# Decay exponents as a bias, a gating norm on another engine, and the order of the last tiles

## The chip, the cores and the metric

The program runs on one core of a Trainium2 chip. The metric is device time in microseconds. The kernel before took 1852.29 us, the median of 3 runs (1849.40 to 1852.42). Engine names are those of the profile: PE is TensorE, DVE is VectorE, ACT is ScalarE, POOL is GpSimd, SP is the engine that issues most DMAs. Each has its own instruction queue and works it off in order.

## The reference

One block of a streaming encoder on a sequence of 1024 rows with 1024 channels, all in float32:

```
x = x + 0.5 * SwiGLU_1(RMSNorm(x))             # hidden width 2816
h = RMSNorm(x);  p = h @ W_in                  # u, v (512 each), q, k, v, z, beta, a
    y_a = gelu(u) * (W_s . layernorm(gelu(v)) + b_s)    # 8 groups of 64 channels, blocks of 128 rows
    y_b = RMSNorm(gated_delta_rule(q, k, v, beta, g)) * silu(z)   # 4 heads of 128, chunks of 64 rows
x = x + concat(y_a, y_b) @ W_out
x = x + 0.5 * SwiGLU_2(RMSNorm(x))
y = RMSNorm(x)
```

Two pieces matter here. In the gated delta rule `decay[i, j] = exp(g_i - g_j)` where j is at or before i, and zero elsewhere, with g the running sum of the gates in a chunk; it is used once below the diagonal (in the matrix L, which a triangular solve inverts) and once with the diagonal (for the attention of the queries). In the spatial gating each row of gelu(v) is normed over its 512 channels, scaled and shifted by `gm_ln_g` and `gm_ln_b`, then mixed over the rows by W_s, and b_s is added.

## The kernel before

Rows stand in tiles of 128 (the partitions), so there are 8 tiles, 0 to 7. Products of float32 are made from a high and a low part in another format: a CAST on ACT makes the high part, a subtraction on DVE the low part (`split`, line 61 and 62, and like lines), and each product takes three matmuls (`mm3`, line 53). A program builder takes the kernel's text and sets, with a cost model of its own, the order in which each engine gets its instructions; the text's order and buffers bound it, and what an engine has been given it works off in that order. So an edit in one place moves instructions elsewhere.

The kernel has three parts. The two feed-forward parts (`ffn`) form products of weight and activation sums on PE, in `plan` order, with hidden values written to DRAM (`hq`) and read back as `left`, and weight sums (`wq`) read back as `right`; `unit` is one such pair, cast and split. The last step of the plan ends four tiles at once: `ev` adds a result into the tile `x` (DVE, line 332), and `emit` norms it. In the first part `emit` is `to_mid` (its result `xn` is transposed by PE), in the second it is `fin`, which writes `o` to the output. Both use `rstd_of` (lines 72 to 78): Square with a sum on ACT, a multiply and add on DVE, a power of -0.5 on POOL (`rpow`, line 70).

The middle part does the mixing. In order of the text:

- `v0` projects half of v; beside it `decay(h)` (lines 786 to 803) makes, for each of four heads, `EL` and `EA`, two tiles E of 128 x 2 x 512. `grb` is the row of g, loaded from DRAM to all partitions into one of four buffers; `gc` is g as a column; `csa` holds the masks (0 or -1e30).
- `keys(h)` projects the keys (`proj_conv`: matmuls into `mm`, a copy to `pad` on ACT, a convolution in four DVE passes into `acc`, Silu on ACT into `kst`), transposes them on PE (`ax<-ident,kst`), norms them (`rk`) and forms L with EL. `fill` puts steps of another projection between.
- `substitute` is the triangular solve for all blocks: 31 steps of two DVE operations each (aT, then X), one behind the other. X is written to DRAM (`xz`) and read back as Z and X by `Half.load`; the PE then needs Z for `inverse`.
- The second half of v is projected; its eviction `ev_v` applies Gelu, and `mix` norms a tile: statistics on DVE, the power on POOL, two DVE passes over 128x512 (lines 1083 and 1084). `spatial` mixes two tiles (a pair) on PE (`ax<-vm,u`), adds b_s on DVE (line 1094) and stores to DRAM. The tiles `vm` and X share three buffers, so the load of pair 2 waits for the store of pair 0.
- The scan over chunks, head by head, with the projections of the next head between.

ACT needs a table load (`ACT_TABLE_LOAD`) when it goes from one kind of function to another: Exp, Silu and Gelu each need one here, copies, casts and Square come without.

## Time and profile before

| what | value |
|---|---|
| median of 3 runs | 1852.29 us (1849.40 to 1852.42) |
| the profiled execution | 1841.22 us, its span 1839.4 us |
| granted PE clock over the span | 0.992 |
| PE busy | 1784.1 us, 97% |
| DVE busy | 1191.7 us, 65% |
| ACT busy | 686.6 us, 37% |
| POOL busy | 747.9 us, 41% |

The span is from the first to the last instruction of the one profiled execution; its own time is 1.8 us longer, and the runs' median 11 us longer than that. Shares are averages over stages that differ: the first feed-forward part lasts until about 700 us, the middle part until about 1080, the second feed-forward part to the end. In a row such as `745.78 5.92 PE ... x35 [2.75 <-DVE wk L62]` the first number is the start in us, the second the length, x35 the merged instructions, and the bracket is how long the engine stood idle before and what ended that. In a row with `679/686/1781` these are the shortest, median and longest duration in ns. In a row of `a:b` the numbers are, for that stretch, the busy time of PE, PEld (weight load), DVE, ACT and POOL, then the clock, the DMA share and GB/s.

### The profile page before, as it was taken

What the parts mean: (1) busy time and instruction counts of PE and PEld (TensorE: products, weight loads), DVE (VectorE), ACT (ScalarE), POOL (GpSimd) and SP (SyncE); (2) the same over time, 40 slices, a digit from 0 to 9 for tenths busy, and PEclk for the clock granted to TensorE, in tenths of its full rate; (3) what the DMA queues carried; (4) which work ended last, traced back from release to release, by engine and by line L of the source; (5) the groups of instructions that cost most, each with busy time, mean ns of one, the idle gap of its engine ahead of it and who ended that gap; (6) DMA issues with size and microseconds to landing.
All of it is one profiled execution on the core that took longest, in us unless ns stands there. A gap on an engine that the chain in (4) does not pass through costs nothing.

```text
span 1839.4 us, 25484 instructions
## 1 busy us (share of the span) xinstructions
PE 1784.1 (97%) x9735; PEld 1524.8 (83%) x9735; DVE 1191.7 (65%) x1531; ACT 686.6 (37%) x1193; POOL 747.9 (41%) x583
## 2 busy tenths in 40 slices
PE   5999999999999999898999999999999999999997
PEld 4888888888788889797788989988888888878886
DVE  6867676665565575769655344587776766656546
ACT  6333332333343454432344533452333323243433
POOL 4667666565140012212132420366666665614001
PEclk9999999999999999999999999999999999999999
DMA  5353443544957445453432254334535445495744
GB/s 196 108 175 136 162 152 134 184 158 163 339 188 258 155 177 164 140 195 100 133 94 67 90 197 136 109 104 165 178 132 171 144 154 188 142 344 185 264 142 149
DMA packets 134441, 302.26 MB, mean 164 GB/s; under 512 B 27408, under 2 KB 42032, under 8 KB 134320
## 3 DMA queue, kind: packets, MB, share of 16 engines
q1 hardware_dynamic: 131824, 296.20, 46.9%
q10 hardware_dynamic: 2496, 4.44, 0.8%
q8 instruction: 76, 1.25, 0.3%
q14 instruction: 45, 0.37, 0.1%
HBM read 208.83 MB, written 91.77 MB: 163 GB/s over the span
## 4 chain that ended last, share of the span: by engine, by line
PE 78%; DVE 8%; DMA 5%; POOL 4%; issue 3%; ACT 2%; SPq 0%; POOLq 0%; DVEq 0%; ACTq 0%
PE mm L53 43%; PE ax L53 32%; POOL s L191 1%; POOL t L278 1%; DMA left<-hq 1%; DVE acc L873 1%; PE ax L95 1%; PE sd L53 1%; DMA graw<-in_f1gu_dram 1%; POOL s L278 1%; PE sc L53 1%; DVE T L119 0%; DVE unit L62 0%; DVE wk L62 0%; DVE E L797 0%
## 5 line engine op out<-in xcount | busy, mean ns | idle before, releaser
L53 PE MATMUL mm<-unit 128*128 128x512 f32 x1056 | 244.9, 392 | 4.2 <-ACT unit L61 2.2
L53 PEld LDWEIGHTS mm<-unit 128*128 128x128 f32 x1056 | 198.8, 189 | 47.4 <-ACT unit L61 3.3
L191 POOL TENSOR_TENSOR s<-graw 128x512 f32<-128x512 f32 x84 | 130.3, 1551 | 262.9 <-DMA graw<-in_f2gu_dram 116.0
L62 DVE TENSOR_TENSOR ga<-graw,ga 128x512 fp32r<-128x512 f32 x134 | 155.9, 1166 | 99.9 <-ACT ga L61 99.2
L61 ACT CAST gs<-s 128x512 fp32r<-128x512 f32 x168 | 104.5, 622 | 301.8 <-PE mm L53 151.0
L62 DVE TENSOR_TENSOR unit<-left,unit 128x1024 fp32r<-128x1024 f32 x84 | 101.9, 1215 | 133.0 <-ACT unit L61 132.3
L53 PE MATMUL ax<-T,gs 128*128 128x512 f32 x792 | 183.1, 389 | 0.0
L53 PE MATMUL ax<-unit 128*128 128x512 f32 x792 | 180.5, 389 | 0.0
L53 PEld LDWEIGHTS ax<-T,gs 128*128 128x128 f32 x792 | 148.7, 188 | 30.8
L53 PEld LDWEIGHTS ax<-unit 128*128 128x128 f32 x792 | 148.7, 188 | 30.8
L62 DVE TENSOR_TENSOR gs<-s,gs 128x512 fp32r<-128x512 f32 x168 | 172.7, 1030 | 2.3
L53 PE MATMUL mm<-B,ga 128*128 128x512 f32 (+1 forms) x864 | 166.8, 347 | 3.3 <-ACT B L118 1.9
L61 ACT CAST unit<-left 128x1024 fp32r<-128x1024 f32 x84 | 82.5, 982 | 230.2 <-PE ax L53 100.5
L53 PE MATMUL mm<-T,gs 128*128 128x512 f32 x720 | 166.5, 389 | 0.0
L53 PEld LDWEIGHTS mm<-B,ga 128*128 128x128 f32 x864 | 139.5, 194 | 23.4 <-ACT B L118 2.5
L53 PEld LDWEIGHTS mm<-T,gs 128*128 128x128 f32 x720 | 135.2, 188 | 28.0
L70 POOL TENSOR_TENSOR rs<-rs,half 128x1 f32<-128x1 f32 (+1 forms) x29 | 19.2, 662 | 334.5 <-DVE rs L76 334.4
L53 PE MATMUL mm<-actT,wk 128*128 128x512 f32 x576 | 150.4, 403 | 0.0
L53 PE MATMUL ax<-B,ga 128*128 128x512 f32 x528 | 127.2, 390 | 1.4 <-DVE ga L62 1.4
L53 PE MATMUL mm<-wk,actT 128*128 128x256 f32 x960 | 123.5, 285 | 2.7 <-DVE wk L62 2.7
L53 PEld LDWEIGHTS mm<-wk,actT 128*128 128x128 f32 x960 | 117.4, 190 | 3.4 <-DVE wk L62 3.0
L53 PEld LDWEIGHTS mm<-actT,wk 128*128 128x128 f32 x576 | 103.6, 188 | 18.8
(239 smaller groups left out, 3046.0 us busy)
## 6 DMA issues: line engine op xcount, KB each, us to landing
left<-hq SPq DMA_DIRECT2D x70, 512.0 KB, 5.0
graw<-in_f1gu_dram SPq DMA_DIRECT2D x44, 512.0 KB, 5.4
wq<-t SPq DMA_DIRECT2D x44, 512.0 KB, 2.8
hq<-s SPq DMA_DIRECT2D x44, 512.0 KB, 3.1
graw<-in_f2gu_dram SPq DMA_DIRECT2D x44, 512.0 KB, 4.7
right<-wq SPq DMA_DIRECT2D x40, 512.0 KB, 4.8
wd<-in_f1wd_dram SPq DMA_DIRECT2D x22, 512.0 KB, 6.6
hq<-sg SPq DMA_DIRECT2D x22, 512.0 KB, 3.7
```

The lines of the kernel that those rows point to most:

```text
L53: nc.tensor.matmul(*args, **kw)
L61: nc.scalar.copy(h, src)
L62: nc.vector.tensor_tensor(l, src, h, op=ALU.subtract)
L70: nc.gpsimd.tensor_tensor(o, i, half[:, :w], op=ALU.pow)
L95: nc.tensor.transpose(ps[:, i * P:(i + 1) * P], blk(i), ident)
L191: nc.gpsimd.tensor_tensor(f, u, v, op=op)
L278: nc.gpsimd.tensor_tensor(o, u, v, op=op)
L873: nc.vector.scalar_tensor_tensor(acc, pad[:, j:j + 512], cw[:, blk, j:j + 1], acc, op0=ALU.mult, op1=ALU.add)
```

## The change

1. Decay: E now holds only mask minus, or plus, the row g, formed in one operation; the column g goes in as the bias of the Exp, which therefore runs on 128 columns at a time. The Exps of EA are placed behind each head's keys.
2. Gating norm: the norm of v is one ACT pass with a bias and a scale column; the channel weights `gm_ln_g` are applied behind the mixing (DVE), and the shift C (from `gm_ln_b`, W_s and b_s) is added there by POOL. C is formed once in `gm_shift`. `gm_consts` moves ahead of `substitute`.
3. The reciprocal root (`rsqrt`) is an addition and a power, both on POOL, with the division by n in the Square's scale; it replaces a DVE operation in `rstd_of`, the keys' norm and `mix`.
4. Last tiles: tile 6's product is returned as a function, to be called later, and tile 7's two halves change places.

```diff
     def rpow(o, i, w):
         nc.gpsimd.tensor_tensor(o, i, half[:, :w], op=ALU.pow)
+    def rsqrt(o, i, add, w=1):
+        nc.gpsimd.tensor_scalar(o, i, add, None, op0=ALU.add)
+        rpow(o, o, w)
     def rstd_of(src, junk, n):
         ms = sm.tile([P, 1], F32, tag="ms", name="ms", bufs=4)
-        nc.scalar.activation(junk, src, AF.Square, accum_out=ms)
+        nc.scalar.activation(junk, src, AF.Square, scale=n ** -0.5, accum_out=ms)
         rs = sm.tile([P, 1], F32, tag="rs", name="rs", bufs=4)
-        nc.vector.tensor_scalar(rs, ms, 1.0 / n, EPS, op0=ALU.mult, op1=ALU.add)
-        rpow(rs, rs, 1)
+        rsqrt(rs, ms, EPS)
         return rs
...
         def fin(t, xt):
             o = gp.tile([P, D], F32, tag="gsp", name="o", bufs=7)
             if t < 7:
-                normed(xt, st["gf"], o)
-                nc.sync.dma_start(odram[t], o)
-                return
-            halves = slice(0, 512), slice(512, D)
+                rs = rstd_of(xt, o, D)
+                def scaled():
+                    nc.vector.scalar_tensor_tensor(o, xt, rs, st["gf"], op0=ALU.mult, op1=ALU.mult)
+                    nc.sync.dma_start(odram[t], o)
+                if t == 6:
+                    return scaled
+                return scaled()
+            halves = slice(512, D), slice(0, 512)
...
     EL, EA = {}, {}
+    ngc = na
+    nc.vector.tensor_scalar(ngc, gc, -1.0, None, op0=ALU.mult)
     def decay(h):
...
-            nc.vector.tensor_tensor(av_, v4(grb), b4(gc[:, cs]), op=ALU.subtract)
-            eng = nc.vector if hf else nc.gpsimd
-            eng.tensor_tensor(lv_, mask(C_ML), v4(grb), op=ALU.subtract)
-            eng.tensor_tensor(lv_, lv_, b4(gc[:, cs]), op=ALU.add)
-            nc.scalar.activation(lv_, lv_, AF.Exp)
-            nc.vector.tensor_tensor(av_, av_, mask(C_MA), op=ALU.add)
-            nc.scalar.activation(av_, av_, AF.Exp)
+            for e, i, eng, op in ((EL[h], C_ML, nc.vector if hf else nc.gpsimd, ALU.subtract), (EA[h], C_MA, nc.vector, ALU.add)):
+                eng.tensor_tensor(v4(e[:, hf]), K(i).unsqueeze(1).to_broadcast([P, 4, P]), v4(grb), op=op)
+
+    def exponents(e, bias, h):
+        for hf in range(2):
+            for t in range(4):
+                c = h * 8 + hf * 4 + t
+                nc.scalar.activation(e[h][:, hf, tl(t)], e[h][:, hf, tl(t)], AF.Exp, bias=bias[:, c:c + 1])
...
-            rk = inv_norm(ssk, 1.0, EPS, "k")
+            rk = small("rk")
+            rsqrt(rk, ssk, EPS, 4)
...
+    def gm_shift(gm):
+        _, C, bs, wsT = gm
+        rows_ = bank(ps_a, "ax")[:, :8]
+        for g in range(8):
+            mm(rows_[:, g:g + 1], wsT[g // 4][:, g % 4], ones, start=True, stop=True)
+        rw = bs[:, 8:16]
+        nc.scalar.copy(rw, rows_)
+        for g in range(8):
+            c = C[:, g * 64:g * 64 + 64]
+            nc.scalar.activation(c, c, AF.Identity, bias=bs[:, g:g + 1], scale=rw[:, g:g + 1])
     def mix(t, v, gm):
...
-        nc.vector.tensor_scalar(rs, mv[:, 1:2], EPS, None, op0=ALU.add)
-        rpow(rs, rs, 1)
-        nc.vector.scalar_tensor_tensor(v, v, mv[:, 0:1], lng, op0=ALU.subtract, op1=ALU.mult)
-        nc.vector.scalar_tensor_tensor(v, v, rs, lnb, op0=ALU.mult, op1=ALU.add)
+        rsqrt(rs, mv[:, 1:2], EPS)
+        nm = mv[:, 0:1]
+        nc.gpsimd.tensor_scalar(nm, mv[:, 0:1], rs, -1.0, op0=ALU.mult, op1=ALU.mult)
+        nc.scalar.activation(v, v, AF.Identity, bias=nm, scale=rs)
     def spatial(t, Vs, gm):
...
-            nc.vector.tensor_tensor(
-                Vs[:, :, gh * 256:gh * 256 + 256].rearrange("p t (g c) -> p g t c", g=4),
-                mp.rearrange("p (g t c) -> p g t c", g=4, t=2),
-                gm[2][:, gh * 4:gh * 4 + 4].unsqueeze(2).unsqueeze(3).to_broadcast([P, 4, 2, 64]), op=ALU.add)
+            o = Vs[:, :, gh * 256:gh * 256 + 256].rearrange("p t (g c) -> p g t c", g=4)
...
+            nc.vector.tensor_tensor(o, mp.rearrange("p (g t c) -> p g t c", g=4, t=2), each(lng), op=ALU.mult)
+            nc.gpsimd.tensor_tensor(o, o, each(C), op=ALU.add)
...
     for h in range(HEADS):
         decay(h)
+        exponents(EL, gc, h)
         together(islice(v0, 2))
...
         keys(h, fill)
+        exponents(EA, ngc, h)
     together(fill)
+    gm = gm_consts()
+    gm_shift(gm)
     substitute()
-    gm = gm_consts()
```

**What the order makes of it.** First place: ACT at the end of the decay and the first head's keys. E are the exponents, wk<-raw the high parts of projection weights, kst<-acc the Silu that ends the convolution of one half of the keys. Before:

```order
L61 CAST wk<-raw 128x1024
L801 ACTIVATE E<-E 128x512
L803 ACTIVATE E<-E 128x512
L801 ACTIVATE E<-E 128x512
L803 ACTIVATE E<-E 128x512 x2
L869 COPY pad<-mm 128x512
L801 ACTIVATE E<-E 128x512
L875 ACT_TABLE_LOAD
L875 ACTIVATE kst<-acc 128x512
L869 COPY pad<-mm 128x512
L61 CAST wk<-raw 128x1024
L896 ACTIVATE kst,ssk<-ax 128x128
```

And of the change (gc is the bias of EL, na that of EA):

```order
L61 CAST wk<-raw 128x1024
L876 COPY pad<-mm 128x512
L810 ACTIVATE E<-E,na 128x128 x12
L882 ACT_TABLE_LOAD
L882 ACTIVATE kst<-acc 128x512
L876 COPY pad<-mm 128x512
L61 CAST wk<-raw 128x1024
L810 ACT_TABLE_LOAD
L810 ACTIVATE E<-E,na 128x128 x7
L882 ACT_TABLE_LOAD
L882 ACTIVATE kst<-acc 128x512
L903 ACTIVATE kst,ssk<-ax 128x128 x8
```

The last Exps of the decay no longer all stand ahead of the first Silu: seven stand between the two Silus of the first head and five more behind them, with a load on either side. Over the program ACT has 20 loads instead of 16.

Second place: PE from the second half of v to the first use of Z. Before:

```order
L53 MATMUL mm<-wk,actT 128x256 x128
L53 MATMUL ax<-vm,u 128x128 x8
L53 MATMUL mm<-wk,actT 128x256 x40
L53 MATMUL ax<-vm,u 128x128 x8
L53 MATMUL mm<-wk,actT 128x256 x24
L53 MATMUL mm<-actT,wk 128x512 x38
L53 MATMUL ax<-vm,u 128x128 x8
L53 MATMUL mm<-actT,wk 128x512 x23
L53 MATMUL ax<-vm,u 128x128 x8
L53 MATMUL mm<-actT,wk 128x512 x83
L53 MATMUL sq<-S,wq 128x128
L53 MATMUL mm<-actT,wk 128x512 x36
```

Of the change:

```order
L53 MATMUL mm<-wk,actT 128x256 x105
L53 MATMUL ax<-vm,u 128x128 x8
L53 MATMUL mm<-wk,actT 128x256 x32
L53 MATMUL ax<-vm,u 128x128 x8
L53 MATMUL mm<-wk,actT 128x256 x42
L53 MATMUL mm<-actT,wk 128x512 x6
L53 MATMUL ax<-vm,u 128x128 x8
L53 MATMUL mm<-actT,wk 128x512 x42
L53 MATMUL ax<-vm,u 128x128 x8
L53 MATMUL mm<-actT,wk 128x512 x96
L53 MATMUL sq<-S,wq 128x128
L53 MATMUL mm<-actT,wk 128x512 x8
```

Ahead of the change's first row stand 13 more of the same and the eight matmuls of `gm_shift`; the row behind each list is the first with Z. The mixings (ax<-vm,u) move forward by 10, 18, then 32 matmuls of 512 columns less, and 152 matmuls of 512 columns stand ahead of Z instead of 180. On POOL, between the norms of the pairs, the change has this (brs and bmv are a tile's scale and bias, the row of vm the two additions of C for one pair):

```order
L74 TENSOR_SCALAR brs<-bmv 128x1
L70 TENSOR_TENSOR brs<-brs,half 128x1
L1102 TENSOR_SCALAR bmv<-bmv,brs 128x1
L1118 TENSOR_TENSOR vm<-vm,rv 128x4x2x64 x2
L74 TENSOR_SCALAR brs<-bmv 128x1
```

The additions of one pair stand ahead of the first operation of the next pair's norm.

Third place: SP in the last step of the plan, where left is read for the last units and o is written. Before:

```order
L648 DMA out_dram<-o 128x1024
L377 DMA left<-hq_10683 128x1024
L648 DMA out_dram<-o 128x1024
L377 DMA left<-hq_10684 128x1024
L648 DMA out_dram<-o 128x1024 x2
L377 DMA left<-hq_10685 128x1024
L377 DMA left<-hq_10686 128x512
L648 DMA out_dram<-o 128x1024 x3
L661 DMA out_dram<-o 128x512
```

Of the change:

```order
L655 DMA out_dram<-o 128x1024
L381 DMA left<-hq_10742 128x1024
L655 DMA out_dram<-o 128x1024 x3
L381 DMA left<-hq_10743 128x1024
L381 DMA left<-hq_10744 128x1024
L381 DMA left<-hq_10745 128x512
L655 DMA out_dram<-o 128x1024 x3
L669 DMA out_dram<-o 128x512
```

The second left now stands behind the outputs of tiles 1 to 3. On DVE the end of the program reads, before, x, o, x, o, x, o, x and the two halves of tile 7; with the change x, x, o, o, x, o, x and the halves: tile 6's product still stands ahead of tile 7's x.

24 lines of the change are left out of this document (11 added, 13 removed).

## The prediction

> **What bounds the kernel now.** I read the page's head first, then who TensorE waits for, then the two stages that the change touches as busy time and in order of time.
>
> ```profile
> span 1839.4 us, 25484 instructions
> PE 1784.1 (97%) x9735; PEld 1524.8 (83%) x9735; DVE 1191.7 (65%) x1531; ACT 686.6 (37%) x1193; POOL 747.9 (41%) x583
> ```
>
> TensorE stands still for 1839.4 - 1784.1 = 55.3 us. The change adds eight matmuls of one column to its work, so it can win or lose only where TensorE waits. TensorE's waits, first between 700 and 765 us (decay and first keys), then between 800 and 900 us (gating norm and triangular solve); columns are total, times, longest:
>
> ```profile
> PE mm L53 <- DVE wk L62: 2.7, 1, 2.7
> PE ax L844 <- ACT kst L875: 2.2, 1, 2.2
> ...
> PE ax L53 <- DVE vm L1084: 4.4, 3, 2.9
> PE ax L53 <- issue: 1.2, 1, 1.2
> PE ax L53 <- DMA Z<-xz: 1.2, 1, 1.2
> ```
>
> These 5 and 6.8 us are what the two large edits can reach. VectorE is nearly full in both stretches (22.75 of 23.00 and 39.93 of 41.83 us):
>
> ```profile
> 722.00:745.00 23.00, 21.03 (x134) 18.92 (x133) 22.75 (x25) 12.18 (x22) 12.27 (x8) 1.00 0.31 97
> 841.00:882.83 41.83, 40.37 (x212) 34.18 (x211) 39.93 (x93) 13.09 (x21) 8.32 (x9) 1.00 0.35 122
> ```
>
> **Decay.** Removed: eight subtractions and eight mask additions on VectorE become eight additions, four of its eight other operations go, and POOL loses four (24 to 12 on VectorE, 8 to 4 on POOL). Added: 64 exponentials of 128 columns for 16 of 512, and, by the order, four table loads, since half of the exponentials now stand between the keys' Silus.
>
> ```profile
> L797 DVE TENSOR_TENSOR E<-grb,gc x8: 679/686/1781, 722.2 to 741.5; 128x512 f32<-128x512 f32 x8
> L799 POOL TENSOR_TENSOR E<-csa,grb x4: 1530/1760/1818, 722.2 to 735.6; 128x512 f32<-128x512 f32 x4
> L1040 ACT ACTIVATE ax<-oh,rq 128x128 f32<-128x128 f32 x32 | 11.9, 372 | 2.4 <-DVE oh L1037 1.8
> 730.99 1.15 ACT L801 ACTIVATE E<-E 128x512 f32<-128x512 f32 x2 [1.08 <-DVE E L800]
> L875 ACT ACT_TABLE_LOAD x2 | 2.6, 1283 | 0.0
> 741.34 1.69 PE L53 MATMUL mm<-wk,actT 128*128 128x256 f32 x13
> 745.78 5.92 PE L53 MATMUL mm<-wk,actT 128*128 128x256 f32 x35 [2.75 <-DVE wk L62]
> 755.52 0.66 PE L844 MATMUL ax<-ident,kst 128*128 128x128 f32 x4 [2.25 <-ACT kst L875]
> ```
>
> No row shows an Exp with a column of biases; the nearest is the Square with a column of scales (L1040), 0.37 us. Two Exps of 0.63 us take 1.15 us, so neighbours overlap by 0.1: 0.27 us each, 64 x 0.27 = 17.3 us against 16 x 0.575 = 9.2. With 4 x 1.28 us of loads, ScalarE gains 13 us of work. If the bias costs nothing it is 0.18 each, the lower bound.
>
> When are the last E ready? POOL's four take 4 x 1.76 = 7.0 us from 722.25; beside them VectorE gets about one operation per 1.5 us, five in all; seven more at 0.69, and a microsecond for the last grb, whose buffer comes free late: 735.3 instead of about 744.6. ScalarE then has, in the new order, four exponentials 1.1, a cast 1.05, eight 2.2, a cast 1.05, the copy of pad 0.6, twelve 3.2, a load 1.28, Silu 0.63: the first kst at 746.4. Then copy 0.6, cast 1.05, load 1.28, seven 1.9, load 1.28, Silu 0.63: the second at 753.1. TensorE finds its wk in time (the casts end at 737.5 and 740.7; VectorE is free), so the 2.75 us go; it waits only for the second kst, and starts those transposes at 753.2 instead of 755.52 with five more matmuls of 0.23 us behind it: 755.5 - 753.2 + 1.2 = **3.5 us won**. Bounds: 5.0 (both waits gone) and 0.5 (ScalarE 3 us later).
>
> [...]
>
> ```profile
> 708.29 1.28 ACT L761 ACT_TABLE_LOAD   x1
> 709.58 0.23 ACT L761 ACTIVATE na<-na 128x32 f32<-128x32 f32 x1
> ```
>
> **Gating norm.** Sixteen VectorE passes of 0.75 us (L1084 below is one) go. In their place ScalarE makes eight passes (0.63 us and the columns: about 0.8), POOL eight small operations more, and, after the mixing, eight additions of 128x512 that follow the product on VectorE. In the order POOL makes both additions of one pair of tiles before it starts the next pair's norm.
>
> ```profile
> L70 POOL TENSOR_TENSOR brs<-brs,half x8: 758/1177/1247, 828.1 to 860.5; 128x1 f32<-128x1 f32 x8
> 815.81 13.82 PE L53 MATMUL mm<-wk,actT 128*128 128x256 f32 x116
> 830.85 2.02 PE L53 MATMUL ax<-vm,u 128*128 128x128 f32 x16 [1.22 <-issue]
> 840.48 2.02 PE L53 MATMUL ax<-vm,u 128*128 128x128 f32 x16 [2.89 <-DVE vm L1084]
> 854.63 2.02 PE L53 MATMUL ax<-vm,u 128*128 128x128 f32 x16 [0.66 <-DVE vm L1084]
> 864.47 19.09 PE L53 MATMUL mm<-actT,wk 128*128 128x512 f32 x83
> 893.16 0.41 PE L53 MATMUL ax<-Z,L 32*32 32x32 f32 x8 [1.17 <-DMA Z<-xz]
> 840.62 0.36 DVE L920 TENSOR_TENSOR aT<-Lb,X 128x192 f32<-128x192 f32 x1
> 849.96 0.75 DVE L1084 SCALAR_TENSOR_TENSOR vm<-vm,brs,rv 128x512 f32<-128x512 f32 x1 [0.43 <-POOL brs L70]
> 882.83 0.33 SPq L923 DMA_DIRECT2D xz<-X  x1
> 820.28 1.28 ACT L1108 ACT_TABLE_LOAD   x1 [4.51 <-PE mm L53]
> ```
>
> TensorE, in before's clock: the new order lets it reach the first mixing ten matmuls earlier, at 828.4; the norm (aggregate at 828, two POOL chains of 0.27 + 0.6 + 0.27, ScalarE 0.8) is done near 831.2: it waits 2.8 (before 1.2). It reaches the second at 836.8; POOL has the first pair's additions until 836, then two chains: 840.4, wait 3.6 (before 2.9). Before the third it needs the low part of a wk that VectorE now makes after six of the solve's operations, two products and two statistics, near 850.2: wait 2.6 (before 0.7). The fourth: none (before 0.8). Sum 9.0 against 5.6.
>
> Behind that stands the solve, a chain on VectorE alone, whose X goes through DRAM: stored at 882.83, and used by TensorE at 893.16, 10.3 us later. In the new order 28 matmuls of 0.23 us, 6.5 us, that ran ahead of this wait stand behind it. So to lose nothing TensorE must pass it at 893.2 - 6.5 = 886.7. Without any wait it would be there at 881.4 (from 815.81: 192 x 0.119, four mixings of 1.8, 152 x 0.23, and 0.6 for the short ones), with 9.0 at 890.4. And X? From 840.62 to 882.83 VectorE takes 42.2 us. Eight passes less their overlap, four waits of 0.43 and four small operations go, 7.3; two convolution passes move behind it, 1.3; dependent neighbours close up, 0.6 back: 34.2 us from 841.4, so 875.6 if POOL leaves VectorE alone. It does not: while POOL ran its six decay operations VectorE's 0.69 us operations took up to 1.78, and six of them needed 8.7 us instead of 3.6, 0.85 us lost for each of POOL's. Six additions lie in this stretch: 5.1, so 880.7, and TensorE gets Z at 891.0. **Lost: 891.0 - 886.7 = 4.3 us.** Bounds: won 0.6 (X at 875.6, the waits 6.1), lost 8.2 (each addition holds VectorE 1.5 us: X at 884.6).
>
> [...]
>
> **The rest.**
>
> ```profile
> 1822.08 0.15 DVE L76 TENSOR_SCALAR rs<-ms 128x1 f32<-128x1 f32 x1 [1.22 <-ACT o L74]
> 1834.06 0.19 POOL L657 TENSOR_SCALAR rs<-rs 128x1 f32<-128x1 f32 x1
> 640.00:680.00 40.00, 40.00 (x197) 33.37 (x197) 30.51 (x40) 21.63 (x33) 4.21 (x6) 1.00 0.40 145
> ```
>
> rs on POOL: the small VectorE operation (0.15 us) becomes one of POOL of 0.19 that stands 0.27 before the power; from Square to product 0.99 for 0.91 us. About four of these lie on TensorE's way (head, second half's start): +0.3. At the end of the first half TensorE never waits between 640 and 680 us, but three x now go ahead of xn on VectorE: +0.2 (0 to 1). The shift of C (eight passes of 64 columns, about 2.4 us) lies in a stretch in which ScalarE waits 4.5 us (820.28): nothing; without that cover, 2.4.
>
> The last tiles:
>
> ```profile
> 1805.17 0.43 SPq L377 DMA_DIRECT2D left<-hq  x1
> 1808.42 1.29 DVE L82 SCALAR_TENSOR_TENSOR o<-x,rs,grow 128x1024 f32<-128x1024 f32 x1 [0.66 <-POOL rs L70]
> 1811.30 1.05 ACT L61 CAST unit<-left 128x1024 fp32r<-128x1024 f32 x1 [0.47 <-DMA left<-hq]
> 1824.16 0.69 DVE L332 SCALAR_TENSOR_TENSOR x<-mm,x 128x512 f32<-128x512 f32 x1
> 1830.99 1.28 DVE L82 SCALAR_TENSOR_TENSOR o<-x,rs,grow 128x1024 f32<-128x1024 f32 x1 [0.73 <-POOL rs L70]
> 1832.19 0.68 DVE L332 SCALAR_TENSOR_TENSOR x<-mm,x 128x512 f32<-128x512 f32 x1
> ```
>
> The order moves only tile 5's x ahead of tile 4's o; tile 6's o still stands ahead of tile 7's x. x of tile 5 comes at 1823.6 instead of 1824.2, and the chain behind it ends 0.4 earlier. But on SP the second left now stands behind the o of tile 3: issued near 1809.0 instead of 1805.2, cast near 1814.8 instead of 1811.3, and needed by TensorE, through cast and subtraction, near 1816.7: +0.8 (0 to 1.5). Together +0.4.
>
> **Sum.** -3.5 + 4.3 + 0.3 + 0.2 + 0.4 = +1.7 us, on the span 1839.4 to 1841.1. The profiled execution took 1841.22 us, 1.8 around its span; the runs' median is 1852.29, 11 us more, so I put the difference on the median: **1854.0 us**.
>
> **Rivals.** *Slower:* POOL's additions hold VectorE for their whole length, the solve ends at 884.6, TensorE starves for Z: +8.2 there, in all +5.6, 1857.9; with the decay's gain at its lower bound +8.6, 1860.9. For it: the E rows and VectorE's 95% in that stretch. Against: VectorE gets in between. It decides from X stored later than 883. *Faster:* the additions fall into VectorE's own waits, X at 875.6: -0.6 there, -4.5 in the decay, nothing at the ends: about -5, 1847. For it: VectorE loses 20 us of work in two stretches that it fills. Against: VectorE stands in order behind TensorE's mixing, which is late. *The last tiles are not reordered as said:* the order shows so; it is in the sum, and if tile 7's x did go first, another 1.4 us would be won.
>
> **Numbers.** 0.2% is 3.7 us, about what can be told from no change. Forecast (the two terms about cancel) 0.39; slower rival 0.36; faster rival 0.25. The range reaches to both: 1844 (both large terms at their best, and 3 us of noise between runs, which spread by that) to 1861. The likeliest case alone: 1850 to 1857.
>
> **What would show it.** Right: the wait on wk near 745 gone, the one on the second kst left at 1 to 3 us; ScalarE's 128x128 Exps near 0.37 us; mixing waits together 7 to 10 us; a wait for Z of up to some microseconds, X stored near 881; VectorE's two-input operations longer beside POOL's additions. Wrong: TensorE waiting for banks or fill behind ScalarE in the decay (then slower), or X stored before 877 and mixing waits under 5 us (then faster).

## The result: 14 us slower, outside the range

| | before | after |
|---|---|---|
| median | 1849.04 us (1842.73 to 1865.67) | 1862.98 us (1856.85 to 1871.34) |
| the profiled execution | 1841.22 us | 1862.39 us |
| its span, clock | 1839.4 us, 0.992 | 1860.5 us, 0.983 |

The ratio is 1.0073, with a 95% interval of 1.0056 to 1.0090: 13.5 us slower, 10.4 to 16.6. The forecast was 1854.0 us, the range ended at 1861. It was put on 1852.29 us, the median of the first three runs of before; with all twenty this median is 1849.04. So the miss is larger in the difference than in the time: +1.7 us were forecast, 13.5 measured. The profiled execution of before lies near the low end of its runs; so the traces differ by 21.1 us where the medians differ by 13.9. The page of after begins:

```profile
span 1860.5 us, 25590 instructions
PE 1799.0 (97%) x9751; PEld 1534.5 (82%) x9751; DVE 1157.8 (62%) x1461; ACT 710.1 (38%) x1262; POOL 764.7 (41%) x638
```

TensorE is still busy for 97%. Of the 21.1 us its idle time makes 6.2 (61.5 us instead of 55.3) and its busy time 14.9, though its work is the same but for eight one-column matmuls. The granted clock of both traces is at every instant 1.00 or 0.50 (in after 1.00 over 880 to 892 us, 0.50 over 896 to 904). A mean of 0.992 is then about 29 us at 0.50 (2 x 0.008 x 1839.4), and one of 0.983 about 63 (2 x 0.017 x 1860.5). These 34 us more at half the clock are up to 17 us of lost work, so waits alone do not explain the result.

TensorE's waits of after, first between 700 and 765 us, then between 800 and 900 us (total, times, longest):

```profile
PE ax L851 <- ACT kst L882: 2.6, 1, 2.6
...
PE ax L53 <- ACT vm L1103: 6.3, 3, 3.5
PE ax L53 <- DMA Z<-xz: 4.2, 1, 4.2
PE ax L53 <- issue: 0.5, 1, 0.5
```

The wait on wk in the decay is gone, as forecast. At the mixing TensorE waits for 6.3 us where 9.0 were forecast. The wait for Z grew from 1.2 to 4.2 us. What stands behind it is seen in TensorE's order of time and in the table of stretches of after (busy time of PE, PEld, DVE, ACT, POOL, then the granted clock, the DMA share, GB/s):

```profile
896.00 0.60 PE L53 MATMUL ax<-Z,L 32*32 32x32 f32 x8 [4.15 <-DMA Z<-xz]
896.53 1.65 PE L53 MATMUL mm<-actT,wk 128*128 128x512 f32 x3
...
908.73 1.91 PE L53 MATMUL ax<-Z,ks 128*128 128x128 f32 x8
```

```profile
880.00:892.00 12.00, 11.85 (x54) 9.48 (x52) 10.41 (x24) 3.43 (x6) 0.29 (x2) 1.00 0.80 257
892.00:896.00 4.00, 0.00 (x0) 0.03 (x1) 2.72 (x4) 2.31 (x4) 0.10 (x1) 0.72 0.24 49
896.00:904.00 8.00, 8.00 (x54) 5.40 (x54) 2.65 (x6) 1.14 (x3) 0.00 (x0) 0.50 0.41 120
904.00:912.00 8.00, 8.00 (x49) 6.31 (x48) 2.42 (x5) 2.05 (x5) 0.19 (x1) 0.57 0.08 14
912.00:960.00 48.00, 47.99 (x437) 39.94 (x436) 24.26 (x57) 20.18 (x50) 14.47 (x18) 1.00 0.31 86
```

During the wait the granted clock falls, and it stays at 0.50 until about 911 us, 15 us after the wait is over. Three matmuls of 128x512 take 1.65 us there; before they took 0.96.

Where the 21.1 us between the two traces arise, by the start of the same matmuls in both (a plus is time that after lost):

| place | us | in the prediction |
|---|---|---|
| head: norms, then a clock of 0.57 for some us | +2.4 | +0.3 with the other norms |
| near 465 us, the same instructions in both | +1.1 | none |
| end of the first half (`to_mid`) | +1.9 | +0.2 |
| decay and keys | -4.1 | -3.5 |
| mixing and solve, up to Z | +7.7 | +4.3 |
| clock at 0.50 behind Z | +5.1 | none |
| near 1620 us, the same instructions in both | +4.5 | none |
| tail | +2.3 | +0.4 |

The line of the solve is worked out as in the prediction: Z's first matmul starts at 896.00 instead of 893.16 (2.84), with 28 fewer matmuls done (28 x 0.227 = 6.35), less the 1.49 us that after was late at the keys' end. The line on the clock: from there (9.2 us late) to the matmuls at 1054.48 before and 1068.80 after (14.3 late). Near 1620 us no instruction is changed. TensorE of before waited 0.23 us for a cast there, that of after 2.36, with a clock of 0.50 from 1634.5 to 1641.3 us behind it; in twelve of the thirteen later traces of this document (after among them), whatever the edit, the wait is 1.6 to 3.1 us. That line is the timing of one execution of before and not the change. So is the line near 465 us: there the thirteen traces lie between 3.3 us less and 1.5 us more than before, whatever the edit.

The rows on which the lines of the head and of the first half's end rest, from TensorE's order of time, first before, then after. At the head ten matmuls took 2.57 us and now 4.07, as the clock fell there (0.57 over 64 to 68 us, 1.00 before). That fall belongs to the execution: the same ten take 2.57 to 2.60 us in four other kernels of this document with the root on POOL, and 3.99 in one without it. These four begin the matmuls behind 1.2 to 1.5 us later than before, which is what the root costs at the head:

```profile
62.67 2.57 PE L53 MATMUL ax<-B,ga 128*128 128x512 f32 x10 [1.42 <-DVE ga L62]
```

```profile
63.65 4.07 PE L53 MATMUL ax<-B,ga 128*128 128x512 f32 x10 [1.75 <-DVE ga L62]
...
653.55 1.25 PE L99 MATMUL ax<-ident,xn 128*128 128x128 f32 x8 [0.58 <-DVE xn L86]
658.52 1.09 PE L99 MATMUL ax<-ident,xn 128*128 128x128 f32 x8 [0.51 <-DVE xn L86]
```

### The profile page after: what moved, and what is told of

Same layout as the page of the kernel before. It is cut to its first block, busy times and chain, and to the rows that moved or that the text cites. A ratio compares the mean times of both kernels' runs of the same rounds, so it can differ in the third digit from the quotient of the medians.

```text
span 1860.5 us, 25590 instructions
## 1 busy us (share of the span) xinstructions
PE 1799.0 (97%) x9751; PEld 1534.5 (82%) x9751; DVE 1157.8 (62%) x1461; ACT 710.1 (38%) x1262; POOL 764.7 (41%) x638
## 5 line engine op out<-in xcount | busy, mean ns | idle before, releaser
L53 PE MATMUL mm<-unit 128*128 128x512 f32 x1056 | 250.7, 398 | 7.4 <-ACT unit L61 4.3
L53 PEld LDWEIGHTS mm<-unit 128*128 128x128 f32 x1056 | 202.6, 193 | 52.6 <-ACT unit L61 5.2
L62 DVE TENSOR_TENSOR ga<-graw,ga 128x512 fp32r<-128x512 f32 x134 | 143.5, 1074 | 112.4 <-ACT ga L61 112.0
L53 PE MATMUL mm<-actT,wk 128*128 128x512 f32 x576 | 155.4, 411 | 0.0
L74 POOL TENSOR_SCALAR rs<-ms 128x1 f32<-128x1 f32 x27 | 15.5, 573 | 325.0 <-ACT xn L79 136.4
L53 PEld LDWEIGHTS ax<-B,ga 128*128 128x128 f32 x528 | 99.8, 189 | 22.9 <-DVE ga L62 2.2
```

The source lines that it names most:

```text
L53: nc.tensor.matmul(*args, **kw)
L62: nc.vector.tensor_tensor(l, src, h, op=ALU.subtract)
L74: nc.gpsimd.tensor_scalar(o, i, add, None, op0=ALU.add)
```

## The experiments

Theory after reading the two traces: the gating norm carries the loss, first by a late X, then by the clock that falls when TensorE stands still; the decay is a gain; root and tail cost a few us. Rivals: the loss lies in the root on POOL and the tail; the clock falls for another reason; X is late because VectorE stands in order behind TensorE, not because of POOL.

### The decay part alone

```diff
+                eng.tensor_tensor(v4(e[:, hf]), K(i).unsqueeze(1).to_broadcast([P, 4, P]), v4(grb), op=op)
...
+                nc.scalar.activation(e[h][:, hf, tl(t)], e[h][:, hf, tl(t)], AF.Exp, bias=bias[:, c:c + 1])
```

> The kernel before with the decay part of the change alone (E formed in one operation, the column as the bias of the Exp, EA's Exps behind the keys). Theory (the decay part is a gain and the loss lies in the gating norm): the wait on wk near 745 us is gone, TensorE is 4.1 us ahead of the kernel before at the end of the keys, as in the changed kernel, and keeps it: 4 us faster than before, ratio 0.998 (0.997 to 0.999). Rival (ScalarE's four added table loads and 64 Exps cost later what they win here): ratio 1.000 or above.

Measured: 1843.83 us, ratio 0.9968 (0.9944 to 0.9992). TensorE of this kernel at the second kst and at Z:

```profile
754.59 0.86 PE L846 MATMUL ax<-ident,kst 128*128 128x128 f32 x4 [3.08 <-ACT kst L877]
...
894.89 0.41 PE L53 MATMUL ax<-Z,L 32*32 32x32 f32 x8 [1.42 <-DMA Z<-xz]
```

No wait on wk is left. The wait on the second kst is 3.08 us, just past the 1 to 3 forecast, and TensorE was slower behind it: the four transposes take 0.86 us, those of the first kst 0.60. So from 716 us, ahead of the decay, to the keys' end this trace gains 1.9 us and not the 4.1 that were expected. The ten traces with the decay part gain 0.9 to 4.1 us there, and after stands at the upper end. The decay part is a gain of its own, by its runs 1.5 to 10 us; the rival falls. ScalarE's part of it, from the trace of after (group of E's Exps with shortest, median and longest in ns, then ScalarE in order of time ahead of the second kst):

```profile
L810 ACT ACTIVATE E<-E,na x32: 387/398/414, 741.9 to 762.6; 128x128 f32<-128x128 f32 x32
```

```profile
752.68 1.28 ACT L810 ACT_TABLE_LOAD   x1
753.98 2.16 ACT L810 ACTIVATE E<-E,na 128x128 f32<-128x128 f32 x7
756.15 1.28 ACT L882 ACT_TABLE_LOAD   x1
757.45 0.63 ACT L882 ACTIVATE kst<-acc 128x512 f32<-128x512 f32 x1
```

Seven Exps take 2.16 us, 0.31 each where 0.27 was forecast. The next activation starts 1.30 us after each load began, in the kernel before 1.29.

### The gating part alone

```diff
+        nc.scalar.activation(v, v, AF.Identity, bias=nm, scale=rs)
...
+            nc.vector.tensor_tensor(o, mp.rearrange("p (g t c) -> p g t c", g=4, t=2), each(lng), op=ALU.mult)
+            nc.gpsimd.tensor_tensor(o, o, each(C), op=ALU.add)
...
+    gm = gm_consts()
+    gm_shift(gm)
     substitute()
```

> The kernel before with the gating norm part of the change alone (norm as one ScalarE pass, channel weights and shift behind the mixing, constants ahead of the solve). Theory: this part carries the whole loss. X is stored about 3 us later than before counted from the keys' end, some 28 matmuls fewer stand ahead of the first use of Z, TensorE waits there for 3 to 5 us, its clock falls to about 0.5 for some 12 us behind that wait: 7.7 + 5.1 = 13 us slower, ratio 1.007 (1.005 to 1.009). Rival (the loss of 14 us comes as much from the root on POOL, the head and the tail): at most 6 us slower, ratio under 1.0035.

Measured: 1866.34 us, ratio 1.0090 (1.0059 to 1.0121), 16.6 us slower. TensorE at Z, and the stretch behind it (clock 0.67 over 40 us; 1.00 in before):

```profile
893.90 0.60 PE L53 MATMUL ax<-Z,L 32*32 32x32 f32 x8 [2.94 <-DMA Z<-xz]
```

The same kernel in the table of stretches:

```profile
880.00:920.00 40.00, 37.06 (x205) 28.14 (x204) 18.09 (x36) 8.61 (x18) 0.58 (x4) 0.67 0.33 94
```

This part alone loses as much as the whole change, or more. The rival's 6 us lie outside the interval. More was lost than the 13 us expected, at the end of the expected range: the clock stayed at 0.50 for 27 us behind this wait, where 12 were expected.

### TensorE kept busy through the wait

The edit, shortened:

```diff
...
+    with tc.issue_after(last):                 # last matmul of the filler
+        wps = bank(ps_a, "ax")
+        for i in range(17):
+            mm(wps, wq_[:, 0, i % 8], hT[0][i % 8 // 4][:, 0, i % 4], start=True, stop=True)
     prep = chain(H[0][0].inverse(), ...)       # behind these
```

> The changed kernel with 17 more matmuls of 128x512 whose result nobody reads (3.9 us at 0.23 us each), placed directly ahead of the first matmul that uses Z, behind the same real matmuls. Theory (the clock falls because TensorE stands still for 4.15 us): the wait for Z nearly goes, the granted clock between 895 and 912 us stays near 1.00 instead of 0.50, and the kernel, with more work, is about 5 us faster than the changed kernel: ratio to the kernel before 1.0045 (1.003 to 1.006). Rival (the clock falls there for another reason, such as the small matmuls of the inverse, or its fall is not what the 5 us are lost to): the clock still falls behind Z and the ratio stays at 1.0073 or above.

Measured: 1856.02 us, ratio 1.0043 (1.0020 to 1.0066). TensorE of this kernel, and the stretch behind:

```profile
887.14 4.01 PE L53 MATMUL ax<-actT,wk 128*128 128x512 f32 x17
892.37 0.41 PE L53 MATMUL ax<-Z,L 32*32 32x32 f32 x8 [1.21 <-DMA Z<-xz]
```

The same kernel in the table of stretches:

```profile
880.00:920.00 40.00, 37.78 (x326) 30.92 (x325) 20.84 (x41) 12.05 (x26) 3.88 (x7) 1.00 0.36 102
```

Seventeen matmuls whose result nobody reads make the kernel about 5.5 us faster than the changed one (1.0073 - 1.0043, times 1848); by the two intervals it can be almost nothing or 11. The traces agree with the 5.5: from the keys' end to the matmuls near 1054 us after loses 12.8 us to before, this kernel 8.3. Z comes no earlier. What changed is that TensorE stood still for 1.21 and, at the next use of Z, 1.01 us and not for 4.15, and that the clock stayed at 1.00. The whole edit also places the inverse behind the projection of v, as the next one does; 153 real matmuls of 512 columns stand ahead of Z instead of 152. That the clock's fall costs some 5 us is shown by this pair together with the trace and the forced orders below; the interval of this pair alone would not carry it.

### Real work in the wait

The edit, shortened:

```diff
-    together(weave(prep, proj_steps(9, wv, values_of(1)), (1,) * 14))
...
+    together(proj_steps(9, wv, values_of(1)))
+    together(islice(first_q, 8))               # 24 matmuls of the next projection
+    last = nc.cur_bb.bb.instructions[-1]
+    with tc.issue_after(last):
+        together(prep)
```

> The changed kernel with 16 more real matmuls (24 in place of 8 of the next projection) forced ahead of the first use of Z, 3.7 us of work that the changed kernel does behind it. Theory (the wait for Z and the clock's fall behind it are the loss): both go, 3.7 + 5 = 8.7 us faster than the changed kernel, ratio to the kernel before 1.0025 (1.001 to 1.004). Rival (these matmuls are missed later, between the dependent steps of the inverse, where TensorE then waits instead): the waits at Pm and Z's steps grow by 3 us or more, and the ratio stays above 1.005.

Measured: 1852.64 us, ratio 1.0019 (0.9999 to 1.0039): 10 us of the 13.5 come back by the order of work alone. TensorE waits 0.32 us for Z, the clock between 880 and 920 us is 1.00, and between the steps of the inverse one wait of 0.59 us is new. The rival falls.

### The additions of C on VectorE, and behind the scan

```diff
-            nc.gpsimd.tensor_tensor(o, o, each(C), op=ALU.add)
+            nc.vector.tensor_tensor(o, o, each(C), op=ALU.add)
```

> The changed kernel with the eight additions of C behind the mixing on VectorE instead of POOL. Theory (POOL's additions hold VectorE and stand ahead of the next pair's norm on POOL): six additions of about 0.7 us join the solve's stretch on VectorE, 4.1 us, but 5 to 8 us of stretched VectorE operations go; X is stored 1 to 4 us earlier counted from the keys' end (70.8 us there), and as 16 more matmuls (3.7 us) stand ahead of Z by its order, the wait for Z is under 1 us and the clock stays at 1.00: 9 us faster than the changed kernel, ratio to the kernel before 1.0025 (1.001 to 1.004). Rival (POOL's additions cost VectorE nothing, the solve is late for its place behind TensorE's mixing): X comes 4 us later, the wait for Z stays at 4 us or more, ratio 1.007 or above.

```diff
-            nc.gpsimd.tensor_tensor(o, o, each(C), op=ALU.add)
...
+        nc.gpsimd.tensor_tensor(m, m, gm[1][:, 0:256], op=ALU.add)      # ev_u0
         nc.gpsimd.tensor_tensor(m, m, e, op=ALU.mult)
...
+        nc.gpsimd.tensor_tensor(y, y, gm[1][:, 256:512], op=ALU.add)    # ev_u1
```

> The changed kernel with the additions of C taken out of the solve's stretch: they stay on POOL but run where the tile is multiplied with gelu(u), behind or beside the scan (16 additions of 128x256 there). Theory: no VectorE operation of the solve is stretched, X is stored 5 to 8 us earlier counted from the keys' end (63 to 66 us instead of 70.8), the wait for Z goes, the clock stays at 1.00, ratio to the kernel before 1.0025 (1.001 to 1.004). Rival (X is late because VectorE stands in order behind TensorE's mixing, not because of POOL): X at the same place, 70 us or more behind the keys' end, the wait for Z and the clock's fall stay, ratio 1.007.

Measured: on VectorE 1846.29 us, ratio 0.9995 (0.9974 to 1.0016); behind the scan 1854.15 us, ratio 1.0056 (1.0035 to 1.0077). First the additions and the solve's second operation in the trace of after, then the solve's two operations in that of the kernel with the additions behind the scan:

```profile
L1118 POOL TENSOR_TENSOR vm<-vm,rv x8: 1294/1330/2746, 834.9 to 875.7; 128x512 f32<-128x512 f32 x8
L930 DVE TENSOR_TENSOR X<-X,aT x31: 183/348/1557, 834.7 to 886.1; 128x31 f32<-128x31 f32 x2, 128x60 f32<-128x60 f32 x2, 128x87 f32<-128x87 f32 x2, 128x112 f32<-128x112 f32 x2
```

```profile
L928 DVE TENSOR_TENSOR aT<-Lb,X x31: 183/351/424, 826.8 to 872.4; 128x31 f32<-128x31 f32 x2, 128x60 f32<-128x60 f32 x2, 128x87 f32<-128x87 f32 x2, 128x112 f32<-128x112 f32 x2
L930 DVE TENSOR_TENSOR X<-X,aT x31: 184/355/426, 829.1 to 873.6; 128x31 f32<-128x31 f32 x2, 128x60 f32<-128x60 f32 x2, 128x87 f32<-128x87 f32 x2, 128x112 f32<-128x112 f32 x2
```

The same operation takes up to 1557 ns beside POOL's additions and at most 426 ns without them. X is stored, counted from the end of the last keys' matmuls:

| kernel | keys' end | X stored | between |
|---|---|---|---|
| before | 814.31 | 882.83 | 68.5 |
| after | 815.80 | 886.61 | 70.8 |
| additions on VectorE | 811.57 | 879.94 | 68.4 |
| additions behind the scan | 810.21 | 874.11 | 63.9 |

So POOL's eight additions cost the solve 6.9 us, 0.86 each, by the stretched operations and by the later mixing together (TensorE's longest wait there is 3.5 us with them, 1.9 without). The same additions on VectorE itself cost 4.5, in an order that is not quite the same (21 matmuls of 512 columns ahead of the third mixing instead of 6). The engine with time to spare was the dearer place. That X would come 5 to 8 us earlier without them is confirmed, and the rival (POOL innocent) falls.

But the kernel behind the scan gained only a third of what I expected. The builder, which knows nothing of these stretches, gave almost the same order of TensorE as in the changed kernel, with the same eight matmuls ahead of Z, and Z still came after them. TensorE of this kernel:

```profile
883.58 0.41 PE L53 MATMUL ax<-Z,L 32*32 32x32 f32 x8 [1.60 <-DMA Z<-xz]
```

The same kernel in the table of stretches:

```profile
880.00:892.00 12.00, 10.40 (x69) 7.10 (x68) 4.90 (x9) 3.61 (x8) 0.10 (x1) 0.68 0.34 91
892.00:896.00 4.00, 4.00 (x15) 2.85 (x16) 0.42 (x1) 0.22 (x1) 0.00 (x0) 0.50 0.04 6
896.00:904.00 8.00, 8.00 (x79) 6.35 (x78) 4.01 (x8) 2.59 (x6) 0.29 (x2) 0.88 0.21 35
```

Behind a wait of 1.60 us the clock fell to 0.50. "No wait for Z, clock at 1.00" was wrong for this run. On VectorE the builder put sixteen more matmuls ahead of Z, there was no wait and the clock stayed, and the kernel was 5.5 us faster than expected. These matmuls, more than X, would make the difference of 0.006 between the two; the second pair under "More work ahead of Z" tests that.

### The root on POOL alone, and with the old tail

```diff
-        nc.vector.tensor_scalar(rs, ms, 1.0 / n, EPS, op0=ALU.mult, op1=ALU.add)
-        rpow(rs, rs, 1)
+        rsqrt(rs, ms, EPS)                     # and the same in the keys' norm
```

> The kernel before with the reciprocal root as addition and power on POOL alone (norms of x and of the keys); nothing else of the change. Theory (read from the traces): TensorE loses 1.2 us at the head, 1.1 us at the first half's end (two waits on xn), and 3.1 us at the tail, since with VectorE's small operation gone the builder puts three x and three o together and the second left of the last sums stands behind three outputs on SP: 1.5 us of wait and 1.6 us at a clock of about 0.57 behind it. In all 5.4 us slower, ratio 1.003 (1.001 to 1.005). Rival (the prediction's own terms: +0.3, +0.2, +0.4): 0.9 us, ratio 1.0005.

```diff
             if t < 7:                          # fin: as before, the rest with rsqrt
...
+                nc.vector.tensor_scalar(rs, ms, 1.0 / D, EPS, op0=ALU.mult, op1=ALU.add)
+                rpow(rs, rs, 1)
```

> The root on POOL as in the run with it alone, but the last eight norms keep the small VectorE operation (multiply and add), whose presence keeps the order of before there: one output between two lefts on SP. Theory (the tail's loss is the second left behind three outputs, set by the order the builder makes without that operation): TensorE's wait near the last 82 matmuls is 0.4 to 0.5 us instead of 1.95, these matmuls take 18.9 us instead of 20.5, so 3.1 us less than the run with the root alone (1.0048): ratio 1.003 (1.001 to 1.005). Rival (the longer root itself delays the last x and o): the wait stays near 2 us and the ratio at 1.005.

Measured: the root alone 1852.62 us, ratio 1.0048 (1.0031 to 1.0065); with the old tail 1851.04 us, 1.0013 (0.9999 to 1.0027). The prediction's 0.9 us for these edits lie below the first interval and inside the second. The waits read from after are there: two on xn of 0.58 and 0.51 us at the first half's end, and 1.95 us in the tail; at the head this trace loses 2.9 us, where the ten matmuls take 4.04 us. The first half's end is the clearest: all seven traces with the root lose 1.8 to 1.9 us there, the six others nothing. Two things were not expected. Beside the old decay the root makes the keys wait 2.6 us longer (kst 3.53, pad 2.87 us), which the changed kernel does not show; and in the profile of the root alone (an execution of 1859.2 us, 6.6 above its median) TensorE waited 1.92 us for Z and lost the clock behind it, with the old tail it waited 1.42 us and did not. So 1.0048 is not the root's share in the changed kernel; by the traces that share is 1.2 to 1.5 at the head, 1.8 at the first half's end and 2.3 at the tail, some 5 us.

I had put the tail's loss down to a left that stands behind three outputs on SP. The order is the cause, but the queue is another, VectorE. In after, VectorE, then TensorE and its clock at that place:

```profile
1824.72 1.28 DVE L654 SCALAR_TENSOR_TENSOR o<-x,rs,grow 128x1024 f32<-128x1024 f32 x1 [0.77 <-POOL rs L70]
1826.77 1.28 DVE L654 SCALAR_TENSOR_TENSOR o<-x,rs,grow 128x1024 f32<-128x1024 f32 x1 [0.77 <-POOL rs L70]
1828.83 1.28 DVE L654 SCALAR_TENSOR_TENSOR o<-x,rs,grow 128x1024 f32<-128x1024 f32 x1 [0.77 <-POOL rs L70]
1830.03 1.22 DVE L62 TENSOR_TENSOR unit<-left,unit 128x1024 fp32r<-128x1024 f32 x1
```

POOL of the same kernel beside the first two of these o:

```profile
1824.77 1.32 POOL L74 TENSOR_SCALAR rs<-ms 128x1 f32<-128x1 f32 x1
1826.16 0.57 POOL L70 TENSOR_TENSOR rs<-rs,half 128x1 f32<-128x1 f32 x1
1826.82 1.32 POOL L74 TENSOR_SCALAR rs<-ms 128x1 f32<-128x1 f32 x1
```

TensorE of the same kernel, in order of time:

```profile
1831.30 20.52 PE L53 MATMUL mm<-unit 128*128 128x512 f32 x82 [1.96 <-DVE unit L62]
```

The same kernel in the table of stretches:

```profile
1832.00:1836.00 4.00, 4.00 (x13) 3.10 (x12) 0.38 (x1) 0.11 (x1) 0.00 (x0) 0.57 0.98 300
```

The cast of that left had been done at 1826.8; its subtraction on VectorE stands behind three o, and each o waits 0.77 us for its root. The root in turn is ready only behind an o: POOL's addition, 0.23 us in its median, starts 0.05 us after the o ahead of it and ends 0.1 us after that o. At 0.23 us the root would be ready before that o ends (an estimate from these rows: 0.05 + 0.23 + 0.1 + 0.57 against 1.28). With the small VectorE operations back, the builder spreads the o as before (TensorE of that kernel):

```profile
1822.07 18.88 PE L53 MATMUL mm<-unit 128*128 128x512 f32 x82 [0.38 <-DVE unit L62]
```

The wait is 0.38 us and the 82 matmuls take 18.88 us instead of 20.52. The edit of the last tiles alone was not run. But the run with the root alone, which lacks that edit, has the same order of x and o on VectorE as the changed kernel, the same wait (1.95 us) and the same slow stretch behind it (20.48 us for the 82 matmuls). What reordered the last tiles was the root.

### Put together without the root

Decay and gating, no root in the norms of x and keys, old tail; the additions behind the scan, then on VectorE:

> The kernel before with the decay part and the gating part of the change, the additions of C behind the scan as in the run before last, and without the root on POOL in the norms of x and the keys and without the edit of the last tiles. Theory: the run with the additions behind the scan less the 5.4 us of root and tail: ratio to the kernel before 0.9995 (0.998 to 1.001); X 63 to 66 us behind the keys' end, no wait for Z above 1 us, so that its gain over the decay part alone (0.9968) could come only from smaller waits at the mixing, which I do not expect. Rival (the root and the tail cost only 0.9 us): 1.002.

> The kernel before with the decay part and the gating part of the change, the additions of C on VectorE, and without the root on POOL in the norms of x and the keys and without the edit of the last tiles. Theory: the run with the additions on VectorE (0.9995) less the root and tail as read from the traces, 1.2 at the head, 1.1 at the first half's end, 3.1 at the tail: 5.4 us, ratio to the kernel before 0.9966 (0.995 to 0.998), with 25 matmuls behind sq and no wait for Z, the clock at 1.00 between 880 and 912 us, 0.4 us of wait in the tail. Rival (the root on POOL is harmless in this arrangement, as the prediction's terms of 0.9 us say): 0.999.

Measured: behind the scan 1850.26 us, ratio 1.0021 (1.0001 to 1.0040); on VectorE 1844.73 us, 0.9979 (0.9964 to 0.9995). The first is what its rival said (1.002), but not for the rival's reason: its profile waits 2.24 us for Z and has a clock of 0.87 over 880 to 920 us, with the tail's wait at 0.37 us as in the kernel before. The second has no wait for Z, a clock of 1.00 there and a wait of 0.37 us in the tail; its ratio lies within the range I gave, 2.4 us above its centre.

### More work ahead of Z

The order of the real-work run, applied to the decay part alone (125 matmuls ahead of Z instead of 119), and to decay and gating with the additions behind the scan (120 instead of 105):

> The kernel before with the decay part alone, and six more real matmuls (125 instead of 119) forced ahead of the first use of Z, where the run with the decay part alone waited 1.42 us. Theory (a wait there is lost, and beyond about 1.5 us halves the clock behind it): no wait for Z, the clock 1.00 behind it in every run, 1.4 us faster than the decay part alone, and the slowest runs (up to 1855 us there) gone: ratio 0.996 (0.994 to 0.998). Rival (these matmuls are missed between the steps of the inverse): waits of 1.4 us or more appear between 892 and 910 us, ratio 0.997 or above.

> The run with decay, gating and the additions of C behind the scan (1.0021, wait for Z 2.24 us and the clock at 0.50 for some 10 us behind it), with 15 more real matmuls forced ahead of the first use of Z. Theory: wait and fall of the clock go, 2.2 + 5 us: ratio 0.998 (0.996 to 1.000), clock 1.00 between 880 and 912 us. Rival (the clock falls there for the small matmuls of the inverse, not for the wait): the clock is at 0.50 again behind Z and the ratio stays at 1.002.

Measured: 1845.10 us, ratio 0.9971 (0.9948 to 0.9995), and 1845.10 us, ratio 0.9972 (0.9954 to 0.9991). For the decay part alone no wait for Z is left and no new one above 0.64 us, the slowest run is 1849.0 us instead of 1855.1, but the median is no better than without the six: a gain of 1.4 us is too small to be told here, and that expectation is neither shown nor refuted. The other pair is clear. TensorE without the forced order, then with it:

```profile
886.36 0.41 PE L53 MATMUL ax<-Z,L 32*32 32x32 f32 x8 [2.24 <-DMA Z<-xz]
```

The same kernel in the table of stretches:

```profile
880.00:920.00 40.00, 37.74 (x322) 30.29 (x321) 19.23 (x39) 12.74 (x28) 3.89 (x7) 0.87 0.30 84
```

```profile
888.32 0.41 PE L53 MATMUL ax<-Z,L 32*32 32x32 f32 x8 [0.76 <-DMA Z<-xz]
```

The same kernel in the table of stretches:

```profile
880.00:920.00 40.00, 39.07 (x341) 31.58 (x340) 23.18 (x45) 14.48 (x30) 4.50 (x9) 1.00 0.33 95
```

The small matmuls of the inverse are the same in both; the clock fell only where TensorE had waited 2.24 us. 9 us come back (1.0021 to 0.9972), more than the 7.2 expected.

Four versions beat the kernel before: the decay part alone, it with more work ahead of Z, and decay and gating without the root, with the additions on VectorE or with more work ahead. Their ratios, 0.9968 to 0.9979, cannot be told apart. So the gating norm, made harmless, brings nothing measurable beyond the decay.

## Why the prediction was wrong, point by point

- **Decay, -3.5 us.** Right in its mechanism and inside its bounds (0.5 to 5.0): -4.1 in the trace, -0.9 to -4.1 in the nine other traces with it, -5.9 (-10 to -1.5) in its own run. The wait on wk went, the second kst was waited for 2.65 us (1 to 3 forecast). That -4.1 lies so close to -3.5 is in part luck. There is a slip in the working of the stage behind it: the row of 116 matmuls at 815.81 was cut off by the window's edge; 128 of them ran from 814.31, so "192 from 815.81" counted 12 matmuls twice and made TensorE's arrival at Z without waits (881.4) 1.4 us too late. The 4.3 us do not rest on it.
- **Gating norm, +4.3 us. This term failed first,** by its size: 7.7, near its own upper bound of 8.2. The place was right (X late, TensorE out of matmuls ahead of Z), the mixing waits were 6.3 instead of 9.0. The eight one-column matmuls of `gm_shift`, put at nothing, held TensorE for 2.3 us ahead of the first mixing (817.58 to 819.87, of which 0.52 wait), which took the place of most of the wait there. X was forecast at 880.7 in before's time and came at 885.1 (886.61 - 1.49), just past the 884.6 of the bound. Counted from the keys' end that is 70.8 instead of 66.4. Of the 4.4 us, 1.8 are the additions: 0.85 us lost for each was the right price (0.86 measured), but eight lie in the solve's stretch, not six. The other 2.6 are in the estimate of the solve without them: 61.3 forecast (875.6 - 814.31), 63.9 measured.
- **Slower rival.** Its point of decision came true (X stored later than 883): I gave it 0.36 and put the forecast elsewhere. Its mechanism holds only in part: it had six additions that hold VectorE for their whole length, 1.5 us each, and it was eight that cost 0.86 each, with 2.6 us from the solve itself. That X came so near its 884.6 is in part luck. And its 1857.9 us, even its 1860.9, were short, since it too had no term for the clock.
- **The clock. This is the term that was missing.** The prediction began from the sentence that the change "can win or lose only where TensorE waits", and I priced the wait for Z as its own length. Of the 21.1 us between the traces 14.9 are busy time and only 6.2 waits. Behind Z TensorE worked at half its clock for 15 us, which costs 5.1 in the trace and about 5.5 in the runs that took the wait's idleness away. With it the sum is 1.7 + 5.1 = 6.8 us, and with the measured size of the gating term 10.2, just below the measured interval; root and tail, some 5 us where 0.9 were forecast, make up the rest.
- **Root, +0.3, and first half's end, +0.2.** Mis-sized: 1.2 to 1.5 and 1.8. The price of the small POOL operation was right in most places (median 229 ns). But eight of its 27 took 1.1 to 1.3 us: two at the head, three at the first half's end and three in the tail, each beside a VectorE pass over 128x1024, as the rows of the tail show above. The group in after:

```profile
L74 POOL TENSOR_SCALAR rs<-ms x27: 222/229/1319, 6.2 to 1851.2; 128x1 f32<-128x1 f32 x27
```

- **Tail, +0.4.** Wrong in the queue and in the size: +2.3. Not the left on SP but the subtraction on VectorE came late, behind three o that each wait 0.77 us for POOL; and again the clock fell behind a wait, this time of 1.96 us.
- **Faster rival.** It needed X at 875.6 and mixing waits under 5 us. The run with the additions behind the scan came nearest, with X 63.9 us behind the keys (878.2 in before's time) and waits of 3.6 us at the mixing. It was still slower than before, since 28 fewer matmuls stood ahead of Z and the clock fell.

No run shows an addition that holds VectorE for 1.5 us, the term of the upper bound: by these runs 0.86 us are lost for each of 1.33 us, with part of the 0.86 due to the later mixing. In the tail it is POOL that took longer: its small addition, started beside a VectorE pass of 1.28 us, takes 1.32 us instead of 0.23.

## What to carry to other kernels

Price a wait of TensorE as its length and the slow stretch behind it (here 4.15 us, then 15 us at a clock of 0.50): where the work ahead of a dependent step runs out, look at the granted clock behind the wait, not only at the wait. When an edit makes a chain look shorter to whatever orders the work, check how much filler that order still leaves ahead of the chain's first use, and pin it there if it is too little. An idle engine is not a free one: an operation moved to POOL beside a chain of VectorE operations cost this chain more than on VectorE itself (the eight additions 6.9 us against 4.5).

## What was not expected of the hardware

**The clock fell after short waits.** TensorE's wait at the first use of Z in each profile, and the granted clock between 880 and 920 us:

| kernel | wait for Z, us | clock |
|---|---|---|
| additions on VectorE, with and without the root; decay alone with more work ahead | 0 | 1.00 |
| real work in the wait | 0.32 | 1.00 |
| additions behind the scan, no root, more work ahead | 0.17 and 0.76 | 1.00 |
| before | 1.17 | 1.00 |
| kept busy | 1.21 and 1.01 | 1.00 |
| decay alone; root with old tail | 1.42 | 1.00 |
| additions behind the scan | 1.60 | 0.83 |
| root alone | 1.92 | 0.83 |
| additions behind the scan, no root | 2.24 | 0.87 |
| gating alone | 2.94 | 0.67 |
| after | 4.15 | 0.79 |

Each row is one execution. In these profiles the clock always fell at 1.60 us and more and never at 1.42 and less, and it stayed at 0.50 for 10 us or more. In four of the five it came back 1.6 to 2.1 us after the first products of 128x128 (`ax<-Z,ks`) began, with the gating part alone only behind the second such group, 27 us after the wait. At the mixing the sixteen products behind nine waits of 2.0 to 3.7 us took 2.6 to 3.6 us (in after 3.48, at a clock of 0.50 from 842.59 to 846.00), those behind the other waits, some of them 2.0 to 2.9 us long, the usual 2.0.

So the length of a wait does not decide alone. TensorE's wait for wo near 1090 us lasts 2.51 us in the kernel with real work in the wait and 2.52 us in before; the clock fell behind the first and not behind the second. The stretch with the wait and the next one of the first kernel, then the two stretches over which the wait lies in before:

```profile
1089.82:1093.24 3.42, 0.91 (x8) 0.82 (x8) 3.36 (x6) 2.56 (x6) 0.00 (x0) 1.00 0.95 347
1093.24:1096.65 3.41, 3.41 (x19) 3.41 (x18) 2.74 (x5) 0.16 (x1) 0.00 (x0) 0.50 1.04 412
```

```profile
1084.70:1088.11 3.41, 2.14 (x15) 1.31 (x13) 3.22 (x6) 3.41 (x8) 0.00 (x0) 1.00 1.02 382
1088.11:1091.53 3.42, 2.04 (x17) 2.04 (x18) 3.42 (x7) 1.43 (x3) 0.00 (x0) 1.00 0.95 355
```

In the first, TensorE is busy for 0.91 of 3.42 us, and the next stretch is at 0.50. In the second it is busy for 2.14 and 2.04 us, and the clock stays at 1.00. So 1.5 us is no threshold but a mark for this place in one execution of each kernel; what sets off a fall is not shown by these runs.

Busy time does not decide alone either. In after TensorE was busy without a pause from 897 to 911 us and the clock stayed at 0.50, while at the mixing (842.59 to 846.00) and in the tail (1832.5 to 1835.8) it was back at 1.00 behind 3.4 us of busy time. That the small matmuls behind Z keep the clock down longer is a reading of this, not a test.
